# A hybrid attention block on one core: the first norm's sums of squares taken from rows of x, seven of eight high parts on ScalarE, and a value tile's weights loaded ahead

## The chip, the cores and the metric

The kernel runs on one core of a Trainium2 chip. The metric is the device time of one execution in microseconds, and the figure compared is the median of several executions. A core has five engines with instruction queues of their own: TensorE (PE in the profile; its weight loads are PEld), VectorE (DVE), ScalarE (ACT), GpSimd (POOL) and SyncE (SP, which here issues nearly all the DMAs). Each takes its instructions in order, and they wait for one another by semaphores.

## The reference, cut to what matters

The reference is one layer of a streaming encoder: a norm, a wide projection, a differential attention beside an mLSTM, a merge, a gated MLP, an embedding term and a last norm, for 1024 tokens of 1024 channels in float32. The change lies in its first lines:

```python
def rmsnorm(x, g):
    xf = x.astype(jnp.float32)
    y = xf * lax.rsqrt(jnp.mean(xf * xf, axis=-1, keepdims=True) + EPS)
    return (y * g.astype(jnp.float32)).astype(x.dtype)

h = rmsnorm(x, norm1_g[i])
z = h @ w_in[i]
qa, ka, va, qk_m, vm, om, if_pre, ga, gb = jnp.split(z, split_pts, axis=-1)
```

The factor of the norm is one number per token. It commutes with the product, so the kernel multiplies x times the gain with the weights first, and applies the factor when it takes a product out of PSUM.

## The kernel before, in words

Activations lie with channels on the 128 partitions and the 1024 tokens along the free axis: x arrives as eight tiles `xt` of 128x1024 (512 KB each). Products keep float32 accuracy by splitting both operands into a high part in a rounded format and the rest: `xh`, `xl` for x, `wh`, `wl` for weights. A product is three matmuls per 128 channels, `xh` by `wh`, `xl` by `wh`, `xh` by `wl` (lines 150 to 152), 512 tokens wide. One output tile of 128 channels by 512 tokens thus takes 24 matmuls over the eight `xt`.

The start is lines 191 to 230. For each `xt` a high part is made (line 209 on ScalarE for tiles 1, 3 and 5, line 211 on VectorE for the other five), then the rest on VectorE (line 212), then the square on ScalarE (lines 215, 218), and VectorE adds six of the squares into two tiles `ss` (line 220). TensorE meanwhile runs the first query tile (`ps_q`, two halves) and the first key tile (`ps_k`, two halves) of head 0, 96 matmuls that need only x and weights. Then `rms_cols` sums `ss` over the partitions with 16 narrow matmuls (line 167; two records each in a trace), VectorE adds the epsilon (line 169), GpSimd raises to the power -1/2 (line 170), and `rms_bcast` spreads the eight columns over the partitions: VectorE makes a diagonal tile `dg` from each column (line 175, two buffers), TensorE multiplies it with ones into `pbc`, ScalarE copies to `rstd` (line 184).

After that the query and key tiles are taken out of PSUM with `rstd` (line 599, `raw`), turned by the rotary tables (SP moves the swapped rows to `sw`, line 602; VectorE lines 603 to 605) and split again (line 121 on ScalarE, line 122 on VectorE). The first value tile `ps_va` (two halves) is evicted by line 268 and transposed on TensorE (line 277, `pt`). The next query tile (head 1) fills the same two PSUM banks as the first, so its first matmul waits for the eviction of the first.

Weights come through `load_w` (lines 128 to 139): a DMA into `wf`, then `wh` on ScalarE and `wl` on VectorE, from pools of three buffers each. A new `wh` waits until TensorE has read the last column block of an older one. Between the steps, `split_ahead` splits later stages' weights (`pr`) and writes them back to memory.

The order in which instructions stand on each engine is not the order of the code: a scheduling layer records the whole program and chooses it, from its own picture of what is ready when. A change in the first lines can move rows far behind them.

Of the kernel before, what the change touches and what calls it, by code (L numbers as in the profile page):

```python
# [11 lines left out]
F32 = mybir.dt.float32  # L12
F32R = mybir.dt.float32r
AF = mybir.ActivationFunctionType
ALU = mybir.AluOpType
# [4 lines left out]
P = 128  # L20
D = 1024
S = 1024
HALF = 512
KD = D // P
NTB = S // P
# [14 lines left out]
LO_YB_LAST = "DDDDDDD"  # L40
LATE_O = True
LATE_D = True
WARM = 12
HI_ACT = (1, 3, 5)
SS_CUT = 6
LO_M = "DDDDDDD"
LO_O = "DDDDDDD"
LO_UP = "DDDDDDD"
# [1 line left out]
EPS = 1e-6  # L50
# [4 lines left out]
T_Q, T_K, T_VA, T_QM, T_KM, T_VM, T_OM, T_GA, T_GB = 0, 4, 8, 12, 16, 20, 24, 28, 36  # L55
# [14 lines left out]
def block_kernel(ctx: ExitStack, tc: tile.TileContext, a: dict, out: bass.AP):  # L70
    nc = tc.nc
    PE, ACT, DVE, POOL, SP = nc.tensor, nc.scalar, nc.vector, nc.gpsimd, nc.sync

    cst = ctx.enter_context(tc.tile_pool(name="cst", bufs=1))
    wp = ctx.enter_context(tc.tile_pool(name="wp", bufs=3))
# [65 lines left out]
    def cut(rhs, c):  # L141
        return [(xh[:, c], xl[:, c]) for xh, xl in rhs]
# [18 lines left out]
    def rms_cols(ss, dst, tbs, name):  # L161

        pcol = mid(f"pcol_{name}")
        n = len(tbs)
        for i, tb in enumerate(tbs):
            for q, part in enumerate(ss):
                PE.matmul(pcol[:, i:i + 1], part[:, i * P:(i + 1) * P], ones[:, 0:1], start=(q == 0), stop=(q == len(ss) - 1))
        ms = cst.tile([P, NTB], F32, tag="rms_ms", name="ms")
        DVE.tensor_scalar(out=ms[:, :n], in0=pcol[:, :n], scalar1=1.0 / D, scalar2=EPS, op0=ALU.mult, op1=ALU.add)
        POOL.tensor_tensor(out=dst[:, tbs[0]:tbs[0] + n], in0=ms[:, :n], in1=mhalf[:, :n], op=ALU.pow)  # L170

    def rms_diag(cols, tbs, pbc):
# [13 lines left out]
    ALL_TB = list(range(NTB))  # L186
    rstd = cst.tile([P, S], F32, tag="rstd", name="rstd1")
    rcol = cst.tile([P, NTB], F32, tag="rcol", name="rcol")
# [5 lines left out]
    first = {T_Q: [], T_K: []}  # L194
    xg = []
    with tc.tile_pool(name="ld", bufs=3) as ld:

        ss = [ld.tile([P, S], F32, tag=f"ss{q}", name="ss1", bufs=1) for q in range(2)]
        for k in range(KD):
            xt = ld.tile([P, S], F32, tag="xt", name="xt", bufs=6)  # L200
            SP.dma_start(out=xt, in_=a["xT"][k * P:(k + 1) * P, :])
            for t, k0 in {0: ((T_Q, 0), (T_K, 0)), 1: ((T_Q, 4),), 2: ((T_K, 4),)}.get(k, ()):
                first[t] += load_w(a["w_in"][t], k0, k0 + 4, lo_eng=DVE)
            if k == 3:
                SP.dma_start(out=ident, in_=a["ident"])
            hi = xp.tile([P, S], F32R, tag="X", name="xh")
            lo = xp.tile([P, S], F32R, tag="X", name="xl")
            if k in HI_ACT:
                ACT.activation(out=hi, in_=xt, func=AF.Copy, scale=v("g1", k))
            else:  # L210
                DVE.tensor_scalar(out=hi, in0=xt, scalar1=v("g1", k), scalar2=None, op0=ALU.mult)
            DVE.scalar_tensor_tensor(out=lo, in0=xt, scalar=v("g1", k), in1=hi.bitcast(F32),
                                     op0=ALU.mult, op1=ALU.subtract)
            if k in (0, SS_CUT):
                ACT.activation(out=ss[k > 0], in_=xt, func=AF.Square)
            else:
                sq = ld.tile([P, S], F32, tag="sq", name="sq")
                ACT.activation(out=sq, in_=xt, func=AF.Square)
                part = ss[k > SS_CUT]
                DVE.tensor_tensor(out=part, in0=part, in1=sq, op=ALU.add)  # L220
            xg.append((hi, lo))

        ahead = {}
        for t in (T_Q, T_K):
            pw = big("ps_k") if t == T_K else None
            ahead[t] = [gemm_part(first[t], cut(xg, half_slice(half)),
                                  pw[:, half_slice(half)] if pw is not None else acc("ps_q"))
                        for half in range(2)]
        rms_cols(ss, rcol, ALL_TB, "n1")
        rms_bcast(rcol, ALL_TB, rstd, "n1")  # L230

    z_order = [T_VA] + [t + h for h in range(1, H) for t in (T_Q, T_K, T_VA)] + [T_VM + h for h in range(H)]
    z_w = {}

    def load_z(t):
        if t in z_order and t not in z_w:
# [330 lines left out]
    with tc.tile_pool(name="att", bufs=1) as at:  # L567
# [214 lines left out]
        for (h, qb), nxt in zip(blocks, blocks[1:] + [None]):  # L782
# [8 lines left out]
            t = transposed(*w, qb)  # L791
# [243 lines left out]
    for n, j in enumerate(OUT_ORDER):  # L1035
        i = j % 4
# [42 lines left out]
    xr = ctx.enter_context(tc.tile_pool(name="xr", bufs=6))  # L1079
# [18 lines left out]
    for j in range(KD // 2):  # L1098
# [3 lines left out]
        for blk, ps in products(merged, o_order(j)):  # L1102
            x, half, whole = x1_adds(j)[blk]
# [6 lines left out]
            else:  # L1110
                sq = ff.tile([P, 2 + HALF], F32, tag="ar", name="sq")[:, 2:]
                ACT.activation(out=sq, in_=x, func=AF.Square)
                tt(DVE, ss2[:, half_slice(half)], ss2[:, half_slice(half)], sq, ALU.add)
        if j == 1:

            tags = (("s1", 1), ("u2", 1)), (("s5", 2), ("s5", 2))
            for k in range(PLE // P):
                ph.append([])
                for half in range(2):
                    if k == 0:  # L1120
                        hi, lo = (half_of(*t, dtype=F32R) for t in tags[half])
                    else:
                        t = ff.tile([P, S], F32R, tag="ac", name="ph", bufs=3)
                        hi, lo = t[:, H0], t[:, H1]
                    t = wp.tile([P, HALF], F32, tag="wf", name="pf")
# [170 lines left out]
    with tc.tile_pool(name="fin", bufs=2) as fp:  # L1296
# [25 lines left out]
        for t0, t1 in PLE_CHUNKS:  # L1322
            n = t1 - t0
            c = slice(t0, t1)
            ss = fp.tile([P, PLE_TOK], F32, tag="ss", name="ss3")
# [47 lines left out]
def _layout(inp):  # L1373
    f = {k: np.asarray(x) for k, x in inp.items()}
    w_in = f["w_in"][0]
# [7 lines left out]
    def put(name, arr):  # L1383
# [19 lines left out]
        "rope_s": np.ascontiguousarray(np.tile(np.concatenate([-sin, sin], 0), (2, 1))),  # L1403
        "lam": np.concatenate([f[n][0] for n in ("lam_q1", "lam_k1", "lam_q2", "lam_k2")]),
        "xT": np.ascontiguousarray(f["x"][0].T),
        "pT": np.ascontiguousarray(f["p"][0, 0].T),
        "w_in": _tiles(w_main),
        "w_g": np.ascontiguousarray(w_in[:, 3584:3592].reshape(KD, P, 8).transpose(1, 0, 2)),
# [25 lines left out]
```

## Time and profile before

| what | value |
|---|---|
| median of 3 executions | 1599.32 us (1598.86 to 1600.32) |
| the profiled execution | 1593.94 us |
| its span in the trace | 1592.2 us |
| TensorE busy | 1543.2 us, 97% of the span |
| VectorE, ScalarE busy | 1264.1 us (79%), 749.4 us (47%) |
| mean granted TensorE clock | 0.991 of full speed |

The span runs from the first instruction to the last one; 1.7 us of the profiled execution lie around it. The profiled execution is 5.4 us below the median of the others. Times within the trace are counted from the start of the span. A granted clock of 1.00 is 2.4 GHz and 0.50 is 1.2 GHz.

### The profile page before, as it was taken

To read this page: it belongs to the slowest core of one execution; us is meant where nothing else is said; L and a number is where in the kernel's file an instruction comes from. 1 tells how busy PE (TensorE), PEld (TensorE's weight loads), DVE (VectorE), ACT (ScalarE), POOL (GpSimd) and SP (SyncE) were. 2 spreads that over 40 slices of the span, in tenths; PEclk is the share of its full clock that TensorE was granted. 3 is DMA by queue.
4 is the path that set the end of the run, shared out by engine and by line. 5 is a ranking of instruction groups with operands and counts; after the bars stand their busy time and mean duration, and the time that the engine had idled before them with its cause. 6 is when DMAs were issued, how large, how long until landed. Compare 5 with 4: busy or idle time off the path is not lost.

```text
span 1592.2 us, 21585 instructions
## 1 busy us (share of the span) xinstructions
PE 1543.2 (97%) x7413; PEld 1272.8 (80%) x7413; DVE 1264.1 (79%) x2196; ACT 749.4 (47%) x1448; POOL 26.0 (2%) x22
## 2 busy tenths in 40 slices
PE   8999999989999999999999999999999899999997
PEld 6777776868788788787788888888888778788997
DVE  6797896586888878759796888888888987878745
ACT  3365553545465564534365444444444634344522
POOL 0000000000000000000000000000000000000000
PEclk8999999999999999999999999999999999999998
DMA  5655655175424232465427333333232765332422
GB/s 182 195 170 177 196 176 178 41 261 170 125 81 132 92 127 86 133 211 189 162 64 242 104 105 108 106 104 102 99 100 99 254 222 192 100 131 60 137 88 89
DMA packets 122652, 222.55 MB, mean 140 GB/s; under 512 B 14448, under 2 KB 28336, under 8 KB 122544
## 3 DMA queue, kind: packets, MB, share of 16 engines
q1 hardware_dynamic: 121968, 220.66, 42.9%
q8 instruction: 58, 0.95, 0.3%
q10 hardware_dynamic: 576, 0.52, 0.1%
q14 instruction: 50, 0.41, 0.1%
HBM read 154.25 MB, written 62.69 MB: 136 GB/s over the span
## 4 chain that ended last, share of the span: by engine, by line
PE 71%; DVE 14%; DMA 7%; issue 4%; ACT 2%; SPq 1%; POOL 0%; DVEq 0%; POOLq 0%; ACTq 0%
PE b L381 18%; PE b L379 18%; PE b L380 18%; PE ps_pg L1334 2%; PE ps_pg L1336 2%; PE ps_pg L1335 2%; DVE cv L875 1%; DVE mg L292 1%; DVE wl L122 1%; PE ps_ya L150 1%; PE ps_ya L151 1%; PE ps_ya L152 1%; DVE T L122 1%; PE pav L756 1%; DVE nmax L729 1%
## 5 line engine op out<-in xcount | busy, mean ns | idle before, releaser
L379 PE MATMUL b<-T,wh 128*128 128x512 f32 x816 | 318.6, 390 | 7.4 <-DVE x L292 3.3
L381 PE MATMUL b<-T,wl 128*128 128x512 f32 x816 | 318.5, 390 | 0.6 <-DVE wl L122 0.6
L380 PE MATMUL b<-T,wh 128*128 128x512 f32 x816 | 317.8, 389 | 0.0
L381 PE MATMUL b<-B,wl 128*128 128x512 f32 x612 | 239.5, 391 | 2.3 <-DVE wl L122 2.2
L379 PE MATMUL b<-B,wh 128*128 128x512 f32 x612 | 239.7, 392 | 0.5 <-ACT wh L121 0.4
L380 PE MATMUL b<-B,wh 128*128 128x512 f32 x612 | 238.6, 390 | 0.0
L121 ACT ACTIVATE wh<-S 128x512 fp32r<-128x512 f32 (+1 forms) x200 | 124.0, 620 | 230.0 <-PE b L380 217.6
L379 PEld LDWEIGHTS b<-T,wh 128*128 128x128 f32 x816 | 153.2, 188 | 42.3 <-ACT T L121 3.6
L381 PEld LDWEIGHTS b<-T,wl 128*128 128x128 f32 x816 | 153.2, 188 | 34.0 <-DVE wl L122 1.9
L380 PEld LDWEIGHTS b<-T,wh 128*128 128x128 f32 x816 | 153.2, 188 | 31.8
L121 ACT ACTIVATE wh<-wr 128x512 fp32r<-128x512 f32 (+1 forms) x150 | 92.8, 620 | 164.6 <-PE b L380 107.6
L122 DVE TENSOR_TENSOR wl<-S,wh 128x512 fp32r<-128x512 f32 (+1 forms) x200 | 134.9, 675 | 39.0 <-ACT wh L121 38.1
L381 PEld LDWEIGHTS b<-B,wl 128*128 128x128 f32 x612 | 114.9, 188 | 28.2 <-DVE wl L122 4.1
L379 PEld LDWEIGHTS b<-B,wh 128*128 128x128 f32 x612 | 114.9, 188 | 24.6 <-ACT wh L121 0.8
L380 PEld LDWEIGHTS b<-B,wh 128*128 128x128 f32 x612 | 114.9, 188 | 23.6
L122 DVE TENSOR_TENSOR wl<-wr,wh 128x512 fp32r<-128x512 f32 (+1 forms) x150 | 101.2, 674 | 7.8 <-ACT wh L121 4.8
L292 DVE TENSOR_TENSOR x<-b,x 128x512 f32<-128x512 f32 x112 | 77.1, 688 | 36.1 <-PE b L381 35.7
L292 DVE TENSOR_TENSOR S<-wr 128x512 f32<-128x512 f32 (+1 forms) x100 | 67.6, 676 | 4.9 <-DMA wr<-w_o 3.4
L1170 DVE SCALAR_TENSOR_TENSOR ac<-ar,vec,ac 128x511 f32<-128x511 f32 (+1 forms) x88 | 65.7, 747 | 0.7
L710 ACT ACTIVATE e<-ps_s,nmax 128x128 f32<-128x128 f32 (+7 forms) x64 | 47.1, 738 | 33.0 <-DVE nmax L729 21.4
L1334 PE MATMUL ps_pg<-x,wpg 128*128 128x384 f32 (+1 forms) x192 | 61.3, 319 | 0.0
L1336 PE MATMUL ps_pg<-x,wpg 128*128 128x384 f32 (+1 forms) x192 | 61.0, 318 | 0.0
(309 smaller groups left out, 2823.9 us busy)
## 6 DMA issues: line engine op xcount, KB each, us to landing
wr<-w_up SPq DMA_DIRECT2D x84, 256.0 KB, 2.8
pre<-pr SPq DMA_DIRECT2D x60, 256.0 KB, 2.4
wr<-w_in SPq DMA_DIRECT2D x56, 256.0 KB, 3.0
wf<-w_in SPq DMA_DIRECT2D x32, 256.0 KB, 3.4
wh<-pre SPq DMA_DIRECT2D x30, 256.0 KB, 3.9
wl<-pre SPq DMA_DIRECT2D x30, 256.0 KB, 4.3
wr<-w_down SPq DMA_DIRECT2D x28, 256.0 KB, 2.8
xt<-xT SPq DMA_DIRECT2D x8, 512.0 KB, 6.4
```

What stands on the lines that cost most here:

```text
L121: ACT.activation(out=hi, in_=src, func=AF.Copy)
L122: (lo_eng or DVE).tensor_tensor(out=lo, in0=src, in1=hi.bitcast(F32), op=ALU.subtract)
L150: PE.matmul(ps, wh, xh, start=(first and k == 0), stop=False)
L292: eng.tensor_tensor(out=out, in0=in0, in1=in1, op=op)
L379: PE.matmul(bank[b], wh, xh, start=(k == 0 and not more), stop=False, **kw)
L380: PE.matmul(bank[b], wh, xl, start=False, stop=False, **kw)
L381: PE.matmul(bank[b], wl, xh, start=False, stop=(k == n - 1), **kw)
L710: ACT.activation(out=e, in_=s_, func=AF.Exp, bias=nm[:, m:m + 1], scale=1.0, accum_out=rs[:, m:m + 1])
L1170: DVE.scalar_tensor_tensor(out=o[:, d:], in0=ar[:, j + d:j + HALF], scalar=v("cf", t * 3 + j), in1=o[:, d:], op0=ALU.mult, op1=ALU.add)
L1334: PE.matmul(pg, wh, xh[:, c], start=(i == 0), stop=False)
L1335: PE.matmul(pg, wh, xl[:, c], start=False, stop=False)
L1336: PE.matmul(pg, wl, xh[:, c], start=False, stop=(i == KD - 1))
```

## The change

The eight squares of `xt` and the six additions go. Instead x is loaded a second time, as rows (128 tokens by 1024 channels, eight tiles `xr` of 512 KB through five buffers), and ScalarE squares each row tile with its accumulator on, which leaves the sum of a token in a column of `ms` without TensorE. Seven of the eight high parts are made on ScalarE, one on VectorE. The two weight pieces of the first value tile are loaded ahead of the rows and are split between the squares. Sixteen instead of twelve matmuls warm TensorE up.

```diff
-WARM = 12
-HI_ACT = (1, 3, 5)
-SS_CUT = 6
+WARM = 16
+HI_ACT = (1, 2, 3, 4, 5, 6, 7)
...
+    def rms_pow(ms, dst, tbs, sums=None):
+        n = len(tbs)
+        DVE.tensor_scalar(out=ms[:, :n], in0=(ms if sums is None else sums)[:, :n], scalar1=1.0 / D, scalar2=EPS,
+                          op0=ALU.mult, op1=ALU.add)
         POOL.tensor_tensor(out=dst[:, tbs[0]:tbs[0] + n], in0=ms[:, :n], in1=mhalf[:, :n], op=ALU.pow)
...
-            if k in (0, SS_CUT):
-                ACT.activation(out=ss[k > 0], in_=xt, func=AF.Square)
-            else:
-                sq = ld.tile([P, S], F32, tag="sq", name="sq")
-                ACT.activation(out=sq, in_=xt, func=AF.Square)
-                part = ss[k > SS_CUT]
-                DVE.tensor_tensor(out=part, in0=part, in1=sq, op=ALU.add)
             xg.append((hi, lo))
+
+        wf_va = [wp.tile([P, 4, P], F32, tag="wf", name="wf") for _ in range(2)]
+        for i, wf in enumerate(wf_va):
+            SP.dma_start(out=wf, in_=a["w_in"][T_VA][:, 4 * i:4 * i + 4, :])
+        rows = []
+        for tb in range(NTB):
+            rows.append(ld.tile([P, D], F32, tag="xr", name="xr", bufs=5))
+            SP.dma_start(out=rows[tb], in_=a["x"][tb * P:(tb + 1) * P, :])
...
-        rms_cols(ss, rcol, ALL_TB, "n1")
+        ms = cst.tile([P, NTB], F32, tag="rms_ms", name="ms")
+        first_va = []
+        for tb in range(NTB):
+            if tb in (4, 6):
+                wh, wl = (wp.tile([P, 4, P], F32R, tag=t, name=t) for t in ("wh", "wl"))
+                split(wh, wl, wf_va[tb // 2 - 2])
+                first_va += [(wh[:, i], wl[:, i]) for i in range(4)]
+            ACT.activation(out=rows[tb], in_=rows[tb], func=AF.Square, accum_out=ms[:, tb:tb + 1])
+        rms_pow(ms, rcol, ALL_TB)
...
-    z_w = {}
+    z_w = {T_VA: first_va}
```

The order of the instructions differs up to about the middle of the attention stage; behind that (6196 of some 7080 matmuls) it is the same on TensorE row by row. Three places matter.

ScalarE, from the fourth tile of x to the end of the norm. Before:

```order
L209 ACTIVATE xh<-xt,vec 128x1024
L218 ACTIVATE sq<-xt 128x1024 x2
L121 ACTIVATE wh<-wf 128x512
L215 ACTIVATE ss_101<-xt 128x1024
L209 ACTIVATE xh<-xt,vec 128x1024
L218 ACTIVATE sq<-xt 128x1024
L121 ACTIVATE wh<-wf 128x512
```

Now:

```order
L120 ACTIVATE wh<-wf 128x512
L211 ACTIVATE xh<-xt,vec 128x1024 x3
L239 ACTIVATE xr,ms<-xr 128x1024
L120 ACTIVATE wh<-wf 128x512
L239 ACTIVATE xr,ms<-xr 128x1024 x2
L120 ACTIVATE wh<-wf 128x512
L239 ACTIVATE xr,ms<-xr 128x1024 x5
```

Five of the eight row squares now stand behind the second `wh` of the value tile. By the semaphores of the built program, the `wh` ahead of the second square waits for the last `xl` matmul of `ps_q`, and the `wh` ahead of the last five for the fourth `xl` matmul of the second half of `ps_k`.

TensorE, where the norm is spread (`pbc`) beside the first half of the value tile. Before:

```order
L176 MATMUL pbc_n_314<-dg,ones 128x128 x2
L150 MATMUL ps_va<-xh,wh 128x512
L176 MATMUL pbc_n_314<-dg,ones 128x128
L151 MATMUL ps_va<-xl,wh 128x512
L152 MATMUL ps_va<-xh,wl 128x512
L150 MATMUL ps_va<-xh,wh 128x512
L176 MATMUL pbc_n_314<-dg,ones 128x128
```

Now:

```order
L149 MATMUL ps_va<-xh,wh 128x512
L150 MATMUL ps_va<-xl,wh 128x512
L151 MATMUL ps_va<-xh,wl 128x512
L180 MATMUL pbc_n_315<-dg,ones 128x128 x4
L180 MATMUL pbc_n_329<-dg,ones 128x128 x4
L149 MATMUL ps_q<-xh,wh 128x512
```

The eight `pbc` matmuls no longer stand between those of the value tile but behind all 24 of its first half, and directly ahead of the query tile of head 1.

VectorE, at the rotary step of the query's second half and the eviction of the value tile (buffer numbers kept: `wl_503` and `wl_492` belong to the second weight piece of head 1's query, `wl_617` and `wl_606` to the first piece of head 1's key). Before:

```order
L122 TENSOR_TENSOR wl_503<-wf_501,wh_502 128x512
L603 TENSOR_TENSOR raw_401<-raw_401,tab_c_387 128x512
L604 TENSOR_TENSOR sw_413<-sw_413,tab_s_388 128x512
L605 TENSOR_TENSOR raw_401<-raw_401,sw_413 128x512
L122 TENSOR_TENSOR ql_400<-raw_401,qh_399 128x512
L268 TENSOR_TENSOR raw_487<-ps_va_462,rstd1_82 128x512
L122 TENSOR_TENSOR wl_617<-wf_615,wh_616 128x512
```

Now:

```order
L121 TENSOR_TENSOR wl_606<-wf_604,wh_605 128x512
L614 TENSOR_TENSOR raw_402<-raw_402,tab_c_388 128x512
L615 TENSOR_TENSOR sw_414<-sw_414,tab_s_389 128x512
L616 TENSOR_TENSOR raw_402<-raw_402,sw_414 128x512
L121 TENSOR_TENSOR ql_401<-raw_402,qh_400 128x512
L279 TENSOR_TENSOR raw_476<-ps_va_451,rstd1_82 128x512
```

The key's weight split stood behind the eviction of the value tile and now stands ahead of the four operations in front of that eviction. Its `wh` waits in both programs for the last `xl` matmul of head 1's query tile, and on TensorE the transposes of the evicted value tile stand one matmul behind that one, in both programs.

## Rows read from the trace of the kernel before

**Rows 1.** The page's busy time of each engine, share of the span, instructions.

```profile
PE 1543.2 (97%) x7413; PEld 1272.8 (80%) x7413; DVE 1264.1 (79%) x2196; ACT 749.4 (47%) x1448; POOL 26.0 (2%) x22
```

**Rows 2.** VectorE by line and form, 0 to 34 us: busy, mean ns, idle before.

```profile
L212 DVE SCALAR_TENSOR_TENSOR xl<-xt,vec,xh 128x1024 fp32r<-128x1024 f32 x8 | 10.2, 1281 | 1.4 <-ACT xh L209 1.4
L220 DVE TENSOR_TENSOR ss<-ss,sq 128x1024 f32<-128x1024 f32 x6 | 7.3, 1219 | 0.0
L211 DVE TENSOR_SCALAR xh<-xt,vec 128x1024 fp32r<-128x1024 f32 x5 | 3.7, 749 | 4.7 <-DMA xt<-xT 4.7
```

**Rows 3.** ScalarE by line and form, 0 to 44 us.

```profile
L218 ACT ACTIVATE sq<-xt 128x1024 f32<-128x1024 f32 x6 | 6.1, 1046 | 2.0 <-DMA xt<-xT 2.0
L209 ACT ACTIVATE xh<-xt,vec 128x1024 fp32r<-128x1024 f32 x3 | 3.4, 1138 | 1.0 <-DMA xt<-xT 1.0
```

**Rows 4.** Timeline, 14 to 44 us: start, duration, instruction, idle before and releaser.

```profile
14.25 1.06 ACT L218 ACTIVATE sq<-xt 128x1024 f32<-128x1024 f32 x1 [1.96 <-DMA xt<-xT]
...
19.84 0.63 ACT L121 ACTIVATE wh<-wf 128x512 fp32r<-128x512 f32 x1 [1.59 <-PE ps_q L151]
...
27.71 4.42 PE L167 MATMUL pcol_n<-ones,ss 128*128 128x1 f32 x30 [0.17 <-DVE ss L220]
...
32.26 1.27 DVE L212 SCALAR_TENSOR_TENSOR xl<-xt,vec,xh 128x1024 fp32r<-128x1024 f32 x1
32.42 2.61 POOL L170 TENSOR_TENSOR rcol<-ms,mhalf 128x8 f32<-128x8 f32 x1 [31.98 <-DVE ms L169]
...
33.67 0.33 SPq L569 DMA_DIRECT2D lamv<-lam  x1
...
37.12 0.40 PE L152 MATMUL ps_q<-xh,wl 128*128 128x512 f32 x1
...
38.94 0.29 DVE L578 TENSOR_TENSOR lp<-lamv 128x128 f32<-128x128 f32 x1 [0.27 <-DMA lamv<-lam]
...
43.06 0.40 PE L152 MATMUL ps_k<-xh,wl 128*128 128x512 f32 x1
```

**Rows 5.** Line 201, the eight 512 KB loads of x: issue to landing.

```profile
DMA to landing us min/median/max: 4.4/6.4/8.2
```

**Rows 6.** Timeline, 46 to 69 us.

```profile
46.14 0.69 DVE L599 SCALAR_TENSOR_TENSOR raw<-ps_q,rstd 128x512 f32<-128x512 f32 x1
...
50.85 0.39 PE L150 MATMUL ps_q<-xh,wh 128*128 128x512 f32 x1
...
50.88 0.69 DVE L603 TENSOR_TENSOR raw<-raw,tab_c 128x512 f32<-128x512 f32 x1 [1.34 <-DMA sw<-raw]
...
59.31 0.69 DVE L605 TENSOR_TENSOR raw<-raw,sw 128x512 f32<-128x512 f32 x1
...
61.43 0.69 DVE L268 TENSOR_TENSOR raw<-ps_va,rstd 128x512 f32<-128x512 f32 x1
...
62.13 0.39 PE L151 MATMUL ps_q<-xl,wh 128*128 128x512 f32 x1
...
62.59 0.60 PE L277 MATMUL pt<-ident,raw 128*128 128x128 f32 x4
...
63.27 0.69 DVE L122 TENSOR_TENSOR wl<-wf,wh 128x512 fp32r<-128x512 f32 x1 [1.15 <-ACT wh L121]
...
68.59 0.33 PE L707 MATMUL ps_s<-kh,qh 64*128 64x128 f32 x2
```

**Rows 7.** Stretches of 2 us: length, busy us of each engine, PEclk, DMA share, GB/s.

```profile
16.00:18.00 2.00, 2.00 (x6) 1.58 (x7) 1.62 (x2) 2.00 (x3) 0.00 (x0) 0.61 1.02 416
18.00:20.00 2.00, 2.00 (x7) 1.57 (x6) 1.47 (x2) 0.41 (x2) 0.00 (x0) 0.54 0.75 289
...
248.00:250.00 2.00, 0.93 (x7) 0.48 (x7) 1.41 (x3) 0.51 (x1) 0.00 (x0) 1.00 0.48 146
...
252.00:254.00 2.00, 2.00 (x6) 1.53 (x5) 0.75 (x2) 1.39 (x5) 0.00 (x0) 0.50 0.48 136
254.00:256.00 2.00, 2.00 (x7) 1.40 (x5) 0.11 (x1) 0.00 (x0) 0.00 (x0) 0.66 0.95 330
```

More of the change, by code (lines that the diff above doesn't have):

```diff
@@ L168, in rms_cols @@
         ms = cst.tile([P, NTB], F32, tag="rms_ms", name="ms")
-        DVE.tensor_scalar(out=ms[:, :n], in0=pcol[:, :n], scalar1=1.0 / D, scalar2=EPS, op0=ALU.mult, op1=ALU.add)
+        rms_pow(ms, dst, tbs, pcol)
+    def rms_pow(ms, dst, tbs, sums=None):
+        n = len(tbs)
+        DVE.tensor_scalar(out=ms[:, :n], in0=(ms if sums is None else sums)[:, :n], scalar1=1.0 / D, scalar2=EPS,
+                          op0=ALU.mult, op1=ALU.add)
         POOL.tensor_tensor(out=dst[:, tbs[0]:tbs[0] + n], in0=ms[:, :n], in1=mhalf[:, :n], op=ALU.pow)
@@ L196, in block_kernel @@
     with tc.tile_pool(name="ld", bufs=3) as ld:
-        ss = [ld.tile([P, S], F32, tag=f"ss{q}", name="ss1", bufs=1) for q in range(2)]
         for k in range(KD):
@@ L1405, in _layout @@
         "xT": np.ascontiguousarray(f["x"][0].T),
+        "x": np.ascontiguousarray(f["x"][0]),
         "pT": np.ascontiguousarray(f["p"][0, 0].T),
```

## The prediction

> **What bounds the kernel now.** I read the page's busy times first. TensorE is busy 97% of the span, VectorE 79%, ScalarE 47% [rows 1]: for most of the span a change pays only where TensorE waits or runs slowly, and the change touches the first 70 us. There I read the groups of VectorE and ScalarE, then the timeline. Three things stand out. VectorE is the late engine of the start: its last `xl` begins at 32.26 and ends at 33.53 [rows 4], long after the loads of x went out. TensorE then spends 27.71 to 32.1 on the narrow matmuls that sum the squares, and the 96 query and key matmuls end only behind 43.06 [rows 4]. And from 46 us on TensorE is full: head 1's query tile begins at 50.85, the value transposes follow at 62.59 without a wait, the first scores at 68.59 [rows 6].
>
> The reader should also see the clock in [rows 7]: the granted clock is 1.00 or 0.50. At 248 to 250 TensorE was busy 0.93 of 2 us and still had 1.00; 252 to 256 then read 0.50 and 0.66. Such an episode costs (1 - 0.50) x 2 + (1 - 0.66) x 2 = 1.7 us; the one at 16 to 20 costs (0.39 + 0.46) x 2 = 1.7 us as well.
>
> **What goes from the start.** VectorE loses six additions of 1.22 us and four high parts of 0.75 us [rows 2], 10.3 us in all. TensorE loses the narrow matmuls, 4.4 us [rows 4]. ScalarE gains four high parts of 1.14 us and loses eight squares of 1.05 us while x arrives [rows 3]. So the data of x are complete earlier. I follow ScalarE's new order:
> - The fourth tile of x lands at 14.25 [rows 4]. Its high part takes 1.14 us and its rest 1.28 us [rows 2, 3]: 16.7. By then TensorE has 30 of the 96 matmuls behind it (counted in its order).
> - ScalarE then waits for a weight buffer, as it did at 19.84 [rows 4]. This comes about 17.6; 0.6 us of split and three high parts, overlapping slightly, end at 21.5, the last `xl` at 22.9 instead of 33.5.
> - From 16.7 on TensorE has work: 66 matmuls at 0.228 us (26 of them lie between 37.12 and 43.06 [rows 4], 5.94 / 26) end at 31.8 instead of 43.4. That is 11.6 us gained, the whole of the change's good.
>
> At this place a rule speaks against the change. A high part costs 1.138 us on ScalarE and 0.749 us on VectorE [rows 2, 3]. The Trainium skill, "ScalarE: Activation LUTs", section "Rules for kernel authors", tells one to put plain multiplications on VectorE; the trace agrees that VectorE is quicker for one instruction. If the four moved ones lay on the path, the sum below would end 4 x 0.39 = 1.6 us higher, at 1601.5. I count them at nothing: the last high part ends at 21.5 and TensorE's backlog reaches to 31.8.
>
> **The norm comes later, not earlier.** `rcol` was ready at 32.42 + 2.61 = 35.0 [rows 4]. Now five row squares stand behind the value tile's second `wh`, and this waits for the 14th last matmul of `ps_k`: 31.8 - 14 x 0.228 = 28.6, with the signal 28.9. The split takes it to 29.6. A square with its accumulator read is not in the trace at this size: at least the 1.05 us of the plain square [rows 3]; taken at 1.25 (a fifth more for the read) at most. I take 1.1, near the plain one: five end at 35.1. Small operation, GpSimd's 2.61 us and signals: `rcol` at 38.3. TensorE has by then run the first half of the value tile, 24 x 0.228 = 5.5, to 37.3, and stands still.
>
> It stands longer than that. Two of the `dg` and the eviction of the query stand on VectorE behind `lp`, which needs `lamv`; `lamv` takes the memory of the row tiles and is issued only after the last square. It took 33.67 to 38.94, 5.27 us, before [rows 4]: 35.2 + 5.3 = 40.5. Four short operations of about 0.29 us (`lp` has 0.29, a `dg` is as large) and the eviction of 0.69 us [rows 6] give 42.6 for head 1's query tile. Before it began at 50.85: still 8.2 us ahead.
>
> The row loads are 4 MB more, in a stretch in which little else is loaded. The last goes out when the third square ends: the value tile's first `wh` waits for the last `xl` matmul of `ps_q`, 32 ahead of the end, 31.8 - 7.3 = 24.5; with signal and split 25.4, and two squares more 27.6. At the bounds of [rows 5], 4.4 and 8.2 us, it lands at 32.0 or 35.8; it is wanted at 34.0. So its cost is 0 to 1.8 us; I take 0, as the median of 6.4 gives 34.0. Behind the waiting row loads SP holds head 1's weight loads, wanted only at 42.6, and `lamv`. The four more warming matmuls cost nothing, since TensorE waits for x up to 16.7; without that cover they are 1.2 us, twice the four transposes of the same size at 62.59 [rows 6], as each takes two passes.
>
> **Where the gain goes.** Head 1's query tile took 50.85 to 62.13, 11.28 us, to its last `xl` matmul [rows 6]. TensorE has idled from 37.3 to 42.6 but for eight short `pbc`; as at 248 to 256 [rows 7] I expect a half clock behind that, 1.7 us. The last `xl` matmul: 42.6 + 11.28 + 1.7 = 55.6, 6.5 us ahead.
>
> Now the VectorE order in the text ahead of this one decides. The key's `wl` used to stand behind the eviction of the value tile; now it stands ahead of the rotary step, and its `wh` waits for the very matmul just named, one matmul ahead of the transposes. So TensorE stands still for the whole chain: `wh` and `wl` (62.13 to 63.27 begins `wl`, 1.14 us), `wl` and two rotary operations of 0.69 each, overlapping to 0.64 (1.9), then line 605 to line 268 (59.31 to 61.43, 2.12, with the high part on ScalarE and `ql` between), then 0.73 for the eviction [rows 6]. Together 5.9 us: the transposes begin at 61.5 instead of 62.59. The rotary step needs its swapped rows as well; from 46.14 to 50.88 [rows 6] that round took 4.7 us, and it starts about 51, so it is ready when the chain comes to it.
>
> After so long a stop the clock falls again, 1.7 us more. From the transposes to the first scores it was 6.0 us [rows 6]; so 61.5 + 6.0 + 1.7 = 69.2 against 68.59. The lead of 8.2 us has become a lag of 0.6 us. Behind this TensorE's order differs in the attention stage without another chain of that kind (many steps on other engines between two neighbouring matmuls), and is the same from its middle on; I carry the shift to the end. The sum against the profiled execution is 1593.94 + 0.6 = 1594.5. That execution lies 5.4 us below the median; on the median it is 1599.32 + 0.6 = 1599.9.
>
> **The rivals.**
> - The clock stays up. For it: TensorE is 97% busy [rows 1], so it waits often for a moment, and the mean clock is still 0.991. Without both episodes the scores come 3.4 us earlier, and some of it is lost to the other branch of the chain (the swapped rows of the key): 1596.7. Against it stands the fall behind 248 to 250 after less idle time than here.
> - The stop ahead of the transposes does not bite, because the weight split's buffer is free earlier than I read, or VectorE's operations overlap more. Then 5.9 us stay and the second clock episode goes: about 1593. Against it: the order is fixed, and every link of the chain is in the rows.
> - Slower: the first tiles come as in the old trace, with waits of TensorE between 12 and 16, and the clock falls at 16 to 20 as it did [rows 7]. Everything behind, squares, `rcol`, `lamv`, moves by 1.7 us; with the last row tile landing late (up to 1.8 us) it is 1599.9 + 3.5 = 1603.4. It decides from the point at which the query and key matmuls end later than 34.4. For it: x lands no earlier than before. Against it: TensorE's idle time between 12 and 16.7 shrinks, as high parts no longer wait behind additions.
>
> **How the numbers follow.** A measurement of this kernel tells about 0.2% from no change, 3.2 us: faster is below 1596.1, slower above 1602.5. My forecast, the lead given back at the transposes, has a chance of 0.50, with a range of its own of 1597.5 to 1602.5; the clock staying up 0.15, half of it below 1596.1; the stop not biting 0.15; the slower case 0.20. Faster: 0.15 + 0.07 and a little for a better order in the attention stage, 0.25. Slower: 0.20 and a little for a worse order there, 0.22. Same: 0.53. The range reaches to the edges of the rivals, 1594.0 to 1603.5. It holds the square's bounds (five times -0.05 to +0.15 us).
>
> **What would show it.** In the profile of the changed kernel: the query and key matmuls end near 32; a gap of TensorE between the first half of the value tile and head 1's query, which begins near 42.6; a second gap of 5 to 6 us ahead of the value transposes, released by VectorE's eviction of the value tile, with ScalarE's `wh` and VectorE's `wl` ahead of it; half clock behind each gap; the first scores near 69. It is wrong if the second gap is under 3 us, if the query and key matmuls end behind 34.4, or if shifts of over 3 us arise behind 70 us.

## The result, and the profile after

The changed kernel takes 1607.19 us (median of 11 executions, 1605.53 to 1616.0) beside 1598.26 us of the kernel before on the same chip (11 executions, 1592.44 to 1605.32). The ratio is 1.0071, with a 95% interval of 1.0056 to 1.0085: about 9 us slower, where the prediction had 1599.9 and an upper end of 1603.5. The profiled execution took 1605.53 us, 11.6 us more than that of before. Two executions of 5414 and 5418 us (one of e1, one of e3) stand outside every ratio below.

The page's busy times of the changed kernel, which answer to [rows 1] (busy us, share of the span, instructions):

```profile
PE 1548.1 (97%) x7389; PEld 1276.1 (80%) x7389; DVE 1254.1 (78%) x2186; ACT 755.1 (47%) x1460; POOL 22.8 (1%) x22
```

VectorE has lost 10 us, TensorE has gained 4.9 us though it has 24 records fewer. The program gives it a little less work (no narrow matmuls of line 167, four more to warm up); it does the work more slowly.

The start first. ScalarE by line and form, 0 to 44 us, which answers to [rows 3] (busy us, mean ns of one, idle time before):

```profile
L239 ACT ACTIVATE xr<-xr 128x1024 f32<-128x1024 f32 x8 | 8.4, 1046 | 1.5 <-DMA xr<-x 1.5
L211 ACT ACTIVATE xh<-xt,vec 128x1024 fp32r<-128x1024 f32 x7 | 7.8, 1146 | 3.3 <-DMA xt<-xT 3.3
...
L239 ACT ACTIVATION_READ_ACCUMULATOR xr<-xr 128x1 f32 x8 | 1.5, 184 | 0.0
```

A row square takes what the plain square of before took. Its accumulator read of 0.18 us lies under the next one: the last five squares begin 1.04 us apart, from 28.57 to 32.73 (the first and the last of them stand in the timeline below).

Timeline of the changed kernel, 28 to 70 us, which answers to [rows 4] and [rows 6] (start, duration, instruction, idle time before and its releaser):

```profile
28.57 1.04 ACT L239 ACTIVATE xr<-xr 128x1024 f32<-128x1024 f32 x1
...
30.78 0.39 PE L149 MATMUL ps_va<-xh,wh 128*128 128x512 f32 x1
...
32.73 1.04 ACT L239 ACTIVATE xr<-xr 128x1024 f32<-128x1024 f32 x1
...
34.15 1.64 POOL L174 TENSOR_TENSOR rcol<-ms,mhalf 128x8 f32<-128x8 f32 x1 [33.71 <-DVE ms L172]
...
38.55 0.29 DVE L589 TENSOR_TENSOR lp<-lamv 128x128 f32<-128x128 f32 x1 [0.35 <-DMA tab_c<-rope_c]
...
40.09 0.50 PE L149 MATMUL ps_q<-xh,wh 128*128 128x512 f32 x1
...
51.54 0.39 PE L150 MATMUL ps_q<-xl,wh 128*128 128x512 f32 x1
...
56.72 0.69 DVE L279 TENSOR_TENSOR raw<-ps_va,rstd 128x512 f32<-128x512 f32 x1
...
57.52 1.09 PE L288 MATMUL pt<-ident,raw 128*128 128x128 f32 x4 [5.36 <-issue]
...
64.92 0.33 PE L718 MATMUL ps_s<-kh,qh 64*128 64x128 f32 x2
...
69.25 0.37 ACT L721 ACTIVATE e<-ps_s,nmax 128x128 f32<-128x128 f32 x1 [2.18 <-DVE nmax L728]
```

The query and key matmuls end where the value tile begins, 30.78. Head 1's query begins at 40.09 instead of 50.85, and its last `xl` matmul at 51.54 instead of 62.13. TensorE then stands still for 5.36 us ahead of the transposes, behind the chain that the prediction names. The first scores come at 64.92 instead of 68.59, the first exponential at 69.25 instead of 72.32. So at 70 us the changed kernel is still 3.1 us ahead.

It loses that, and 9.4 us more, in the stages of the first heads. I cut both traces at the first exponential of heads 0 to 3. Stretches of the kernel before (length, then busy us of PE, PEld, DVE, ACT, POOL, then PEclk, DMA share, GB/s):

```profile
72.32:118.94 46.62, 45.84 (x259) 34.68 (x258) 43.37 (x93) 29.02 (x74) 2.45 (x1) 1.00 0.55 167
118.94:177.79 58.85, 57.40 (x337) 46.21 (x336) 48.23 (x103) 32.98 (x87) 2.01 (x2) 1.00 0.58 176
177.79:238.57 60.78, 59.55 (x351) 48.18 (x350) 52.03 (x108) 34.30 (x86) 4.12 (x3) 1.00 0.61 190
```

The same of the changed kernel:

```profile
69.25:118.80 49.55, 49.23 (x250) 35.80 (x249) 41.05 (x89) 28.92 (x73) 1.33 (x1) 1.00 0.45 138
118.80:182.32 63.52, 60.75 (x348) 49.64 (x347) 49.61 (x106) 35.02 (x91) 2.01 (x2) 0.97 0.57 175
182.32:247.96 65.64, 59.87 (x344) 48.12 (x343) 52.04 (x108) 33.14 (x84) 2.97 (x3) 0.97 0.57 181
```

The three stages are 178.71 us instead of 166.25, 12.5 us longer. Length less PE busy is TensorE's idle time: 0.32, 2.77 and 5.77 (8.9 in all) instead of 0.78, 1.45 and 1.23 (3.5), so 5.4 us of the 12.5. The clock of 0.97 is one half-clock episode of 3.4 us in each of the last two stages, 1.7 us each, 3.4 us. What is left, 3.7 us, is TensorE busy for longer at full clock: 3.4 us of it lie in head 0, where TensorE is idle for 0.32 us in all (in head 1 it is 1.6 us more, in head 2 1.4 us less). It is more for the same work: seven key matmuls of head 1, of 0.23 us each, stood behind the first exponential before and stand ahead of it now, which makes the stretch 1.6 us shorter. So TensorE is slower by about 5.3 us. Behind head 3 the changed kernel has two half-clock episodes more than before, and its span ends 11.5 us later.

What TensorE does for longer is the scores. Stretches of head 0 with the score matmuls alone (`ps_s`: length, busy us of PE, PEclk, DMA share, GB/s), before and changed:

```profile
72.32:118.94 46.62, 11.12 (x66) 1.00 0.55 167
69.25:118.80 49.55, 16.05 (x66) 1.00 0.45 138
```

The same 66 matmuls take 4.9 us more. In heads 1 and 2 they take 1.3 us more and 0.5 us less, 5.7 us more in all. The reason is seen where they stand. A score contracts over 64 channels; the two maps of a head lie on the two halves of the 128 rows, and each score matmul uses one half. Timeline of TensorE before:

```profile
142.10 0.49 PE L707 MATMUL ps_s<-kh,qh 64*128 64x512 f32 x2
142.44 0.39 PE L707 MATMUL ps_s<-kl,qh 64*128 64x512 f32 x2
142.66 0.40 PE L707 MATMUL ps_s<-kh,ql 64*128 64x512 f32 x2
```

And in the changed kernel, in head 0:

```profile
73.41 0.39 PE L718 MATMUL ps_s<-kl,qh 64*128 64x512 f32 x1
73.73 0.33 PE L759 MATMUL pt<-ident,e 128*128 128x128 f32 x1
73.99 0.49 PE L718 MATMUL ps_s<-kl,qh 64*128 64x512 f32 x1
74.00 0.50 PE L718 MATMUL ps_s<-kh,ql 64*128 64x512 f32 x1
74.43 0.49 PE L767 MATMUL pav<-va,wT 128*128 128x128 f32 x2
74.85 0.49 PE L718 MATMUL ps_s<-kh,ql 64*128 64x512 f32 x1
```

Before, the two matmuls of a row (x2) begin within 4 ns of each other, and the next row begins 0.22 us later: two halves in the time of one. In the changed kernel transposes (pt) and products (pav) of all 128 rows stand between them: the scores at 73.41 and 74.85 run alone, and only those at 73.99 and 74.00 beside each other. A change between 64 and 128 rows may cost a little too: the first row behind one lasts 0.34 us to the next (142.10 to 142.44), the second 0.22; but the first row behind a wait lasts as long (40.09 to 40.43 in the changed kernel), so these rows do not show a price of the change by itself. The Trainium skill, "TensorEngine Tiling (Array Packing)", section "Key Properties", says that tiles operate independently, and that changing the tiling mode drains TensorE; these rows agree with the first, by the 4 ns, and do not settle the second.

And the waits that came: VectorE of the changed kernel in head 2, with the TensorE row that waits for it:

```profile
200.53 0.17 DVE L749 RECIPROCAL rr<-rsum 128x2 f32<-128x2 f32 x1 [0.70 <-ACT e L721]
...
203.38 0.21 DVE L751 SCALAR_TENSOR_TENSOR cc<-rsum,neglam,rr 128x1 f32<-128x1 f32 x1
...
204.89 0.53 DVE L753 SCALAR_TENSOR_TENSOR e<-e,cc 128x384 f32<-128x384 f32 x1
...
205.57 0.52 PE L759 MATMUL pt<-ident,e 128*128 128x128 f32 x3 [2.45 <-DVE e L753]
```

Before, the three operations stood behind each other:

```profile
193.53 0.17 DVE L738 RECIPROCAL rr<-rsum 128x2 f32<-128x2 f32 x1 [0.38 <-ACT e L710]
193.73 0.22 DVE L740 SCALAR_TENSOR_TENSOR cc<-rsum,neglam,rr 128x1 f32<-128x1 f32 x1
193.99 0.62 DVE L742 SCALAR_TENSOR_TENSOR e<-e,cc 128x384 f32<-128x384 f32 x1
```

The combination of the two maps begins 0.46 us behind the reciprocal before, and 4.36 us now, as a rotary step, evictions and splits of the next head stand between them.

### The profile page after: what moved, and what is told of

The parts are those of the page before. It is cut to its first block, busy times and chain, and to the rows that moved or that the text cites. A ratio compares the mean times of both kernels' runs of the same rounds, so it can differ in the third digit from the quotient of the medians.

```text
span 1603.7 us, 21536 instructions
## 1 busy us (share of the span) xinstructions
PE 1548.1 (97%) x7389; PEld 1276.1 (80%) x7389; DVE 1254.1 (78%) x2186; ACT 755.1 (47%) x1460; POOL 22.8 (1%) x22
## 4 chain that ended last, share of the span: by engine, by line
PE 77%; DVE 10%; DMA 6%; issue 3%; ACT 3%; POOL 0%; SPq 0%; DVEq 0%; POOLq 0%; ACTq 0%
PE b L392 18%; PE b L390 18%; PE b L391 18%; PE ps_s L718 2%; PE ps_pg L1345 2%; PE ps_pg L1347 2%; PE ps_pg L1346 2%; DVE cv L886 1%; PE pav L767 1%; DVE mg L303 1%; PE ps_ya L149 1%; PE ps_ya L150 1%; PE ps_ya L151 1%; DVE wl L121 1%; DMA pr<-w_up 1%
## 5 line engine op out<-in xcount | busy, mean ns | idle before, releaser
L1345 PE MATMUL ps_pg<-x,wpg 128*128 128x384 f32 (+1 forms) x192 | 61.3, 319 | 0.0
L1347 PE MATMUL ps_pg<-x,wpg 128*128 128x384 f32 (+1 forms) x192 | 61.0, 318 | 0.0
L1346 PE MATMUL ps_pg<-x,wpg 128*128 128x384 f32 (+1 forms) x192 | 61.0, 318 | 0.0
```

The source lines that it names most:

```text
L1345: PE.matmul(pg, wh, xh[:, c], start=(i == 0), stop=False)
L1346: PE.matmul(pg, wh, xl[:, c], start=False, stop=False)
L1347: PE.matmul(pg, wl, xh[:, c], start=False, stop=(i == KD - 1))
```

## The experiments

My theory behind the result: the order of the instructions in the head stages costs the time, not the start. Rivals: the start (its stop of 5.36 us and what it shifts), the row loads, or chance of the clock. All ratios are to the kernel before on the same chip, with 95% intervals.

**e1_after_again.** The changed kernel once more, for its level beside the next three.

> The changed kernel once more, for a second profile of it beside the others. Theory O (the order of the three head stages costs the time): the stages of heads 0 to 2, from first exponential to first exponential, again take about 49.5, 63.5 and 65.6 us (before: 46.6, 58.9, 60.8), with TensorE idle at the same places; time about 1607. Theory C (the clock happened to fall more often in the one profile): the stages of heads 1 and 2 come back to within 2 us of 58.9 and 60.8 where the clock doesn't fall.

1610.42 us, ratio 1.0093 [1.0073, 1.0112]. The loss is there again. This run has no rows to show, so it does not decide between the two theories; e3 does, which has the loss with 1.7 us of half clock in its stages instead of 3.4.

**e2_new_start_old_order and e3_old_start_new_order.** The two factors crossed: the start of one kernel with the order of the other behind the first scores. The order is fixed by a chain of edges between neighbours on each engine, numbered from the end of the program:

```diff
+ORDER = {"PE": "...", "DVE": "...", "Activation": "...", "SP": "..."}
+def _pin(nc, tc):
+    ...
+        for p, q in zip(row, row[1:]):
+            tc.add_manual_dep(q, p.name, mybir.DependencyInfo(
+                mybir.DependencyClass.NoSync, mybir.DependencyReason.DATA), reason="order")
...
         block_kernel(tc, aps, out)
+        _pin(nc, tc)
```

> The changed kernel's start, and from the first scores on the order of the kernel before on TensorE, VectorE, ScalarE and SyncE. Theory O: the start's lead of 3 to 4 us at the first exponential stays, the head stages take 46.6, 58.9 and 60.8 us, the time is 1599 - 3 = about 1596, ratio 0.996 to 0.999. Theory S (the new start itself, its row loads or its clock, costs the time later): still about 1607, ratio near 1.007.

> The kernel before's start, and from the first scores on the order of the changed kernel. Theory O: it loses what the changed kernel loses there and has no lead to set against it, 12.5 - 0.6 us, about 1599 + 11 = 1610, ratio 1.006 to 1.009. Theory S: no change, about 1599.

e3: 1.0066 [1.0047, 1.0085]. The old start with the new order has the whole loss; its stages are 50.3, 63.5 and 62.8 us. Of the 10.3 us by which they are longer than before, 3.6 are idle time of TensorE, 1.7 half clock and 5.0 TensorE busy for longer, here with the same wide matmuls as before: the parts shift from one execution to the next. e2: 1.0065 [1.0046, 1.0083], a miss for the theory at first sight. Its stages of heads 1 and 2 are 59.5 and 60.8 us, those of before; but head 0 takes 53.8, with a stop of TensorE of 4.65 us at 80 that neither kernel has, and a half clock behind it. ScalarE stood there behind one high part (`pr`) that waited 4.94 us for its load, ahead of the exponentials. The seam, where the new start meets the old order, was at fault, and e6 repeats the run without it.

**e4_three_places.** The changed kernel with its largest waits in heads 1 and 2 taken out by hand: at three places VectorE's row maxima, or the combination, ahead of rotary and split operations, at one place ScalarE's exponentials ahead of splits. In head 2, for one:

```diff
 L749 RECIPROCAL rr<-rsum 128x2
+L751 SCALAR_TENSOR_TENSOR cc<-rsum,neglam,rr 128x1
+L753 SCALAR_TENSOR_TENSOR e<-e,cc 128x384
 L614 TENSOR_TENSOR raw<-raw,tab_c 128x512
...
-L751 SCALAR_TENSOR_TENSOR cc<-rsum,neglam,rr 128x1
...
-L753 SCALAR_TENSOR_TENSOR e<-e,cc 128x384
```

> The changed kernel with its own order, but for three places of heads 1 and 2 on VectorE and one on ScalarE: the row maxima of the 768-key blocks of heads 1 and 2 ahead of the rotary step and of the norm's second step, and the combination of the 384-key block of head 2 ahead of the rotary step. Theory O, sharpened to these three waits of TensorE (1.6 + 0.6, 2.5, and 0.9 + 1.7 us idle, and the two falls of the clock behind them, 1.7 us each): 6 to 10 us faster than the changed kernel, ratio to the kernel before 0.999 to 1.003. If the loss is spread over many small waits instead: 2 to 4 us faster than the changed kernel, ratio about 1.005.

1604.25 us, 1.0052 [1.0035, 1.0069]. The stages are 49.1, 62.6 and 63.6 us: 3.5 us came back of 12.5, nearly all of it as the two half clocks of 1.7 us, which did not come here. What TensorE waited for in heads 1 and 2 of the changed kernel (us in total, times, longest):

```profile
PE ps_s L718 <- ACT e L721: 4.8, 4, 1.7
PE pt L759 <- DVE e L753: 2.4, 1, 2.4
...
```

and in e4:

```profile
PE pav L767 <- ACT wT L760: 2.5, 5, 1.4
PE pt L759 <- DVE e L753: 1.9, 3, 0.8
PE ps_s L718 <- ACT e L721: 1.7, 2, 1.2
...
```

With the two smaller groups of each, 8.5 us of waits became 7.1, at other places: most of what I took out came back elsewhere. Beside e1, on the same chip, e4 is 6.2 us faster by the medians, the lower end of what I expected of these waits; in the profiled executions the spans of e4 and the changed kernel are the same, 1603.9 and 1603.7 us. Its ratio is still that of a loss.

**e5_no_weights_ahead.** The changed kernel without the one edit that loads and splits the value weights ahead; the scheduling layer is free.

```diff
-        wf_va = [wp.tile([P, 4, P], F32, tag="wf", name="wf") for _ in range(2)]
-        for i, wf in enumerate(wf_va):
-            SP.dma_start(out=wf, in_=a["w_in"][T_VA][:, 4 * i:4 * i + 4, :])
...
-            if tb in (4, 6):
-                ...
-    z_w = {T_VA: first_va}
+    z_w = {}
```

> The changed kernel without one of its edits: the value tile's weights are neither loaded ahead of the rows nor split between the squares; row squares, seven high parts on ScalarE and 16 warming matmuls stay. The order that comes out keeps the pairs of score matmuls of head 0 together (16896 columns of TensorE time one after the other, as in the kernel before; 23808 in the changed kernel). Theory O (the order of the head stages costs the time): the stages of heads 0 to 2 come within 2 us of 46.6, 58.9 and 60.8 where the clock stays up, ratio 0.994 to 1.001. Theory S (row loads, high parts on ScalarE or the lower clock cost the time): ratio 1.005 to 1.009.

1595.81 us, 0.9987 [0.9973, 1.0001]. The loss is gone. The layer now chooses for the head stages nearly the order of before; stages of 48.6, 58.7 and 63.4 us, the first and the last with 1.7 us of half clock in them. This is the edit that turned the order.

**e6_old_order_mended and e7_spare_tiles.** e6 is e2 with that one `pr` moved behind the exponentials of 512 keys. e7 is e6 with a shorter chain ahead of the transposes: the value tile's first eviction goes to a spare buffer, and the first key half is turned ahead of the second query half. The move of e6:

```diff
 L721 ACTIVATE e,rsum<-ps_s,nmax 128x256 x2
 L120 ACTIVATE kh<-raw 128x512
-L120 ACTIVATE pr<-pr 128x512 x2
+L120 ACTIVATE pr<-pr 128x512
 ...
 L721 ACTIVATE e,rsum<-ps_s,nmax 128x512
+L120 ACTIVATE pr<-pr 128x512
```

> The run with the new start and the old order once more, with one row of ScalarE moved at the seam: the high part of a weight split that waited for its load and held up the exponentials of the 384-key block (TensorE stood for 4.65 us there) goes behind the exponentials of the 512-key block. Theory O: 5 to 8 us faster than with the seam, head 0 from first exponential to first exponential 46 to 48 us where the clock stays up, ratio 0.998 to 1.002. Theory S: as with the seam, 1.0065, the time only moves elsewhere.

> As the run with the old order mended, and the first value eviction goes to a spare tile (one of the exponentials' buffers) instead of waiting for the query's, the first key's swapped rows to two spare tiles, with the key's first half turned ahead of the query's second. If the chain of rotary steps ahead of the value transposes is what takes the start's lead (TensorE stood 5.4 us there in the changed kernel): TensorE does not stop there, the first scores stand at 58 to 60 instead of 65, no fall of the clock behind, 6 to 8 us faster than the mended run, ratio 0.992 to 0.996. If the head stages are bound by VectorE: the scores come earlier, but the end of head 0 does not, and the time is that of the mended run.

e6: 1598.89 us, 1.0002 [0.9985, 1.0019]. With the order of before the whole of the change costs nothing, and brings nothing: its first exponential was 1.5 us ahead of before, head 0 took 48.0 us instead of 46.6. e7: 1.0022 [1.0005, 1.0040], a miss. Its first scores came at 60.24, 8.4 us ahead of before, and then TensorE stood still for longer than ever:

```profile
70.03 0.63 ACT L120 ACTIVATE pr<-pr 128x512 fp32r<-128x512 f32 x1 [3.69 <-DMA pr<-w_ya]
...
70.69 0.69 DVE L121 TENSOR_TENSOR pr<-pr 128x512 fp32r<-128x512 f32 x1 [3.63 <-ACT pr L120]
71.30 0.68 DVE L279 TENSOR_TENSOR raw<-ps_va,rstd 128x512 f32<-128x512 f32 x1
...
72.03 1.11 PE L288 MATMUL pt<-ident,raw 128*128 128x128 f32 x4 [10.63 <-DVE raw L279]
```

The value tile's second eviction now stood behind the split of a later stage's weight, whose load had been issued at 66.92. I had moved the stop, not removed it.

**e8_pairs_broken and e9_halves_apart.** Both take the kernel before and change nothing but where the score matmuls stand in 26 groups of six. In e8 three of one half come ahead of three of the other; in e9 one matmul of all 128 rows stands between the threes as well.

```diff
 L707 MATMUL ps_s_1054<-kh_424,qh_399 128x512
+L707 MATMUL ps_s_1054<-kl_425,qh_399 128x512
+L707 MATMUL ps_s_1054<-kh_424,ql_400 128x512
 L707 MATMUL ps_s_1055<-kh_424,qh_399 128x512
-L707 MATMUL ps_s_1054<-kl_425,qh_399 128x512
 L707 MATMUL ps_s_1055<-kl_425,qh_399 128x512
-L707 MATMUL ps_s_1054<-kh_424,ql_400 128x512
```

> The kernel before with its own order on every engine, but in 26 groups of six score matmuls the three of one row half stand ahead of the three of the other, instead of in turn. If two neighbouring score matmuls of different row halves run side by side and cost the time of one (as their starts 3 ns apart say): 17536 more columns one after the other at 0.226 us for 512, 7.7 us, ratio 1.003 to 1.005, a part of it hidden where TensorE waits. If the pairing costs nothing: no change, ratio 0.999 to 1.001.

> The kernel before; in 26 groups of six score matmuls of heads 0 to 3 (the same groups as in the run with the neighbours reordered), one matmul that uses all 128 rows now stands between the three of the upper half of the rows and the three of the lower half. Counted in the order, the columns that run with no matmul of the other half beside them rise from 60416 to 89344. Theory (halves that have a full-width matmul between them run one after the other, and this is a part of what the new order costs, where this count is 69504): 28928 columns at 0.226 us per 512 are 12.8 us more, ratio 1.008; TensorE's time in the stages of heads 0, 1 and 2 without idle time and half clock rises from 45.9, 57.4 and 59.5 us by about 2.0, 3.8 and 3.8. Rival (the halves still run beside each other, as when only neighbours were reordered; the new order's cost is waits alone): 1.000 to 1.001, these times unchanged.

e8: 1598.04 us, 1.0003 [0.9986, 1.0020], a miss for the theory as I had put it. TensorE is busy for 45.9, 57.4 and 60.4 us in the three stages instead of 45.8, 57.4 and 59.6: 0.9 us more where I had counted 7.7. In most groups the halves still ran beside each other: the second half's first matmul at 140.83 started 10 ns behind the first half's first, though two more of the first half stood ahead of it. A few groups in head 2 ran apart. e9: 1607.32 us, 1.0066 [1.0044, 1.0087]. Its stretches between first exponentials:

```profile
72.57:121.73 49.16, 49.12 (x259) 35.82 (x258) 43.55 (x93) 28.94 (x74) 2.45 (x1) 1.00 0.53 160
121.73:182.99 61.26, 61.26 (x335) 47.63 (x334) 48.20 (x103) 33.28 (x88) 2.02 (x2) 1.00 0.56 169
182.99:246.54 63.55, 63.55 (x351) 49.65 (x350) 52.42 (x108) 34.32 (x85) 2.97 (x3) 1.00 0.57 182
```

TensorE is busy for 173.9 us instead of 162.8, 11.1 us more, with the same matmuls, and all of it lies in the scores (41.0 us instead of 29.9); the order gives 22016 more columns without a neighbour in these three heads, at 0.226 us per 512 of them 9.7 us. Its idle time went from 3.5 us to nothing, so that 7.7 us remain on the stages' length. By the same count the changed kernel has 6912 more such columns in head 0 and 2176 in head 1: 4.0 us, where its scores take 5.7 us more. So the neighbours that were lost explain most of what TensorE is slower by, a part of the cost that needs no wait at all. The count falls 1.4 and 1.7 us short; what it leaves out is that the matmuls change more often between 64 and 128 rows (60 times in the three stages before, 72 in the changed kernel, 100 in e9). No run takes the two apart.

**e10_no_weights_old_order and e12_no_weights_mended.** Rows and high parts without the weights ahead, behind the first scores the order of before; e12 with the `pr` moved as in e6.

> The changed kernel without the value weights loaded ahead, and behind the first scores the order of the kernel before, pinned. Theory (the order of the head stages sets their length, a lead at the start lasts if that order has no wait more): first exponential at 67.8 as without the weights, stages of 46.6 to 48.6, 58.9 and 60.8 us, so 2 to 4 us ahead of before at the fourth head and at the end, ratio 0.997 to 0.9985. Rival (the lead is given back whatever the order, in waits for other engines and in half clock behind them): stages as long as the lead, ratio 0.9995 to 1.001.

> The changed kernel without the value weights loaded ahead, with the order of before behind the first scores, and one high part of a later stage's weights (ScalarE, pr) moved behind the exponentials of 512 keys, so that it no longer waits for its load at 76 to 81 us ahead of them. Theory (the stop of 5.4 us and the half clock of 17.1 us behind it, 8.5 us, are all that kept the pinned order at 1.005; a lead at the start lasts under the old order, as the run with the high parts alone shows): first exponential at 67.8 to 71.4, stages of 47 to 48, 59 and 61 us, ratio 0.997 to 0.9995. Rival (the rows of x cost something of their own in later stages): stages longer than 48.5, 59.5 or 61.5, ratio 1.001 or more.

e10: 1605.45 us, 1.0050 [1.0032, 1.0068], a miss: I had left in the seam of e2. ScalarE and TensorE of e10:

```profile
81.09 0.63 ACT L120 ACTIVATE pr<-pr 128x512 fp32r<-128x512 f32 x1 [5.04 <-DMA pr<-w_ya]
...
83.06 0.80 PE L759 MATMUL pav<-va,wT 128*128 128x128 f32 x2 [5.44 <-ACT wT L752]
```

The clock read 0.50 from 81 to 98, though TensorE was busy again from 83. e12: 1597.36 us, 0.9999 [0.9983, 1.0016]. One high part at another place of ScalarE's queue is worth 8 us here and 10 us between e2 and e6. But the lead did not last either: the first exponential came at 68.31, 4.0 us ahead, and head 0 took 50.3 us, with 2.7 us of idle time and 1.5 us of half clock. At head 1 0.3 us were left of the lead, and the ratio lies between those of the theory and of the rival.

**e11_high_parts_only.** The kernel before with one edit. The order behind the norm stays as it was on every engine.

```diff
-HI_ACT = (1, 3, 5)
+HI_ACT = (1, 2, 3, 4, 5, 6, 7)
```

> The kernel before with one edit: seven of the eight high parts of x on ScalarE; squares of x, additions and narrow matmuls stay, and the order of the head stages stays that of before. Theory (this edit is not what turned the order): ratio 0.998 to 1.001; the query and key matmuls end 0 to 3 us earlier, as VectorE loses 4 x 0.75 us. Rival (the four high parts lie on ScalarE's path at the start, between squares, 4 x 1.14 us more): the start 1 to 3 us later, ratio 1.001 to 1.002.

1593.62 us, 0.9977 [0.9961, 0.9993]: faster than both kernels, by 3.5 us against before, a little more than I had expected at best. Its stretches:

```profile
68.50:115.21 46.71, 45.97 (x259) 34.73 (x258) 43.39 (x93) 29.06 (x74) 2.44 (x1) 1.00 0.55 171
115.21:174.39 59.18, 57.41 (x337) 46.17 (x336) 48.11 (x103) 33.01 (x87) 2.01 (x2) 1.00 0.58 175
174.39:235.91 61.52, 59.57 (x352) 48.19 (x351) 51.93 (x108) 34.16 (x85) 4.12 (x3) 1.00 0.60 189
```

The first exponential comes 3.8 us earlier than before, that of head 3 still 2.7 us. So a lead at the start lasts through these heads, where the order behind it is the same and no new stop arises. That it lasts to the end is carried by the medians alone: the profiled execution's span is 1597.6 us, longer than the 1592.2 of before, at a mean clock of 0.986 instead of 0.991. The clock at 16 to 20, where before read 0.61 and 0.54 [rows 7], stayed at 1.00 here. It did so in e3 and e8 as well, which have the start of before: whether it falls there changes from one execution to the next. The first exponential of e8 came at 71.00, so that some 1.3 us of the lead of 3.8 here, and of the changed kernel's 3.1, are the clock's.

## Why the prediction was wrong

- **The start, to the first scores: right, with sizes off to the good side.** The query and key matmuls ended at 30.8 (predicted 31.8), squares at 33.8 (35.1), `rcol` at 35.8 (38.3), as GpSimd took 1.64 instead of 2.61 us. `lp` began at 38.55 (40.5), head 1's query tile at 40.09 (42.6, though the terms given add up to 42.4). The high parts on ScalarE cost nothing, as counted; the first row square waited 1.5 us for its load, the last five for none.
- **The clock behind the first gap: wrong.** I had taken 1.7 us; the clock read 1.00 from 36 to 42, with TensorE busy 1.6 of 2 us at 36 to 38 and 38 to 40. That episode was missing, and the tile's last `xl` matmul began at 51.54 instead of 55.6: 2.5 us from the earlier start, 1.5 us from the clock. In e2, where this gap was longer (TensorE busy 1.56 and 0.93 of 2 us from 38 to 42), the clock did fall, from 42.6 to 46.0.
- **The stop ahead of the transposes: right.** From that `xl` matmul to the transposes 5.98 us (predicted 5.9), 5.36 of them idle, by the very chain (`wl` at 52.68, the last rotary operation at 54.61, the eviction at 56.72), and a half clock at its end:

```profile
56.00:58.00 2.00, 0.48 (x3) 0.52 (x4) 1.97 (x3) 0.48 (x1) 0.00 (x0) 0.77 0.41 95
58.00:60.00 2.00, 2.00 (x7) 1.71 (x6) 0.69 (x3) 0.60 (x1) 0.00 (x0) 0.50 0.67 216
```

- **The first scores: too early for the forecast.** They came at 64.92 instead of 69.2: a lead of 3.7 us where I had a lag of 0.6. The errors of the start all went one way, and should have made the kernel faster than forecast.
- **The step that failed** is the one behind it: "Behind this TensorE's order differs in the attention stage without another chain of that kind ..., and is the same from its middle on; I carry the shift to the end." The shift was -3.1 us at 70 us and +9.4 us at 248. I looked in the new order for one long chain between neighbours on TensorE. There is none, and there need not be. The cost is spread, in the profiled execution: 5.4 us of short waits for VectorE's and ScalarE's own order, 3.4 us of half clock, and 3.7 us of TensorE busy for longer, about 5.3 for the same work, most of it score matmuls without a neighbour of the other half. e3 has the loss with the old start, e6 has none of it with the new start: the order costs it, and the start does not. e5 and e12 keep the row loads and lose nothing. e5 shows which edit brought the order.
- **A part of it stood in the rows.** The pairs ran two for one in the trace of before, and the two orders could be counted: 60416 columns without a neighbour against 69504, times 0.226 us per 512, 4.0 us slower by the count. I had not asked what in the old order made it quick.
- **The rivals.** All three spoke of the start. None had the order of the head stages as its mechanism; I gave a worse order there 0.02. (The second, 5.9 and 1.7 us below 1599.9, comes to 1592.3, not 1593.) The prediction had named "shifts of over 3 us behind 70 us" as what would make it wrong, and this is what came.
- **Still open.** Why the layer turns the order of heads 0 to 2 when the first value weights come early; e5 shows that it does. And why rows and weights give back their lead in head 0 even under the old order (e6, e12), where the high parts alone keep theirs (e11): in e12 TensorE waits there up to 0.9 us at a time for ScalarE's and VectorE's rows, and I did not take these waits apart.

## What to carry to other kernels

When a scheduling layer or a planner chooses the order, an edit is paid for wherever the order changes, and a reordered stretch is to be costed like a new edit: count what ran side by side, and what now stands ahead of the operation that TensorE waits for. Cross the start of one kernel with the order of the other before looking for single waits; taking out the largest waits brought back 3.5 of the 12.5 us of these stages. Compare stretches of equal work: a cut at an event in the trace can leave matmuls on the other side of it. Try the parts of a change alone: here one constant out of four edits gave the only gain clear of noise.

## What the runs showed of the hardware that was not expected

- Score matmuls on the two halves of TensorE's rows overlap although other matmuls of the first half stand between them in the queue (e8, starts 10 ns apart); one matmul of all 128 rows between them ends it (e9, +11.1 us busy in the three stages of heads 0 to 2).
- In a stop of 5.36 us, which ended at 57.52, the clock of the changed kernel fell, and read 0.50 from 57.1 to 60.5. In one of 5.44 us, which ended at 83.06, that of e10 fell, and read 0.50 from 81.0 to 98, with TensorE busy 14.94 of the last 15 us. Around the first exponential of e12 it read 0.50 from 67.8 to 71.2 with TensorE busy 3.25 of 3.40 us, behind 64.0 to 67.8 with 2.92 of 3.8 us busy.
- GpSimd's power of 128x8 numbers took 1.64 us in the changed kernel and in e11, 2.61 us before and in e3, e8 and e9. Why is open.
